# Batched trace of A·B: the uneven share of one load of B, 1,568 columns in five pieces instead of 800 in four

## The chip, the cores and the metric

The kernel runs on one core of one Trainium2 chip. The metric is the device time of the program in microseconds; the time before is 707.16 us, the median of three runs (707.16 to 707.89).

## The reference

For each of 8 pairs of 2176 x 2176 float32 matrices, the trace of the product is computed:

```python
B, N = 8, 2176
prod = np.matmul(a, b)                                    # a, b: [B, N, N] float32
traces = np.diagonal(prod, axis1=1, axis2=2).sum(axis=-1)
return traces.astype(np.float32)                          # [B]
```

The trace of A·B is the sum over all i, k of A[i, k] · B[k, i]. So no matrix product is needed: A is transposed, multiplied element by element with B, and summed.

## The kernel before

The rows of a matrix are cut into three groups: two of six rows a partition (6 x 128 rows each) and one of five (5 x 128). Partition p of a group holds r consecutive rows. Three large buffers in bfloat16 receive the loads: `a_six` (both groups of six of A), `b_six` (the same of B) and `five` (the group of five, of A and of B in turn). `at` holds A transposed, in the layout of B.

All large loads are issued from GpSimd's queue (POOL) by the helper `fetch` (line 179), and they cast float32 to bfloat16 on the way. For each batch `n` the order is: the five rows of A into `five`, the twelve rows of A into `a_six`, the five rows of B into `five`, the twelve rows of B into `b_six`. POOL waits before an issue until the buffer is free. `product` (line 188, 211) counts the products on VectorE that have been read out of `five` and `b_six`; `made` counts the tiles that TensorE has transposed.

TensorE transposes A in tiles into three PSUM slots (L253 and L256). ScalarE (L295) copies three of every four tiles into `at`, VectorE (L319) the fourth. VectorE then multiplies `at` with the five and with the six rows of B and sums along the free axis (L308), in place. The loop over `n` in which VectorE does this waits for `b6_full[n]`, the full count of the loads of `b_six` of that batch (line 329). The last batch is different: its B comes in ten pieces, part of which TensorE multiplies (L282) and sums on the diagonal.

Each load of 128 partitions is spread over the core's 16 DMA engines, and each engine counts 1 on the load's semaphore when its part is done.

The load of `b_six` in the fourth batch (`UNEVEN = 3`) differs from the others. `cut` is the place in each row block of 6 x 2176 = 13056 columns where the last `NARROW` columns begin. The load up to `cut` covers all 128 partitions; the last `NARROW` columns of both groups are loaded in pieces, one for each number in `COUNTS`, which is how many partitions it covers. The sum of `COUNTS` is 128, and all pieces together load the same bytes as the one load in the other batches:

```python
if n == UNEVEN:
    cut, p0 = SIX * N - NARROW, 0
    fetch(d_b6, dst[:, :, :cut], src[:, :, :cut])
    for count in COUNTS:
        p1 = p0 + count
        fetch(d_b6, dst[p0:p1, :, cut:], src[p0:p1, :, cut:])
        p0 = p1
else:
    fetch(d_b6, dst, src)
b6_full.append(d_b6.count)
```

Of the kernel before, what the change touches and what calls it, by code (L numbers as in the profile page):

```python
# [21 lines left out]
def kernel(  # L22
# [12 lines left out]
    TWICE = 2 * SIX  # L35
    assert TWICE + FIVE == NT
    LAST = BATCH - 1
    UNEVEN, NARROW, COUNTS = 3, 800, (13, 70, 9, 36)
    assert sum(COUNTS) == P and UNEVEN < LAST

    bf16 = mybir.dt.bfloat16
# [367 lines left out]
```

## Time and profile before

| | before |
|---|---|
| median of 3 runs | 707.16 us (707.16, 707.89, 707.16) |
| profiled execution | 707.1 us, span 705.3 us |
| HBM read | 303.04 MB, 430 GB/s over the span |
| VectorE busy | 385.8 us (55%) |
| ScalarE busy | 204.9 us (29%) |
| TensorE busy (matmul) | 198.9 us (28%) |
| GpSimd busy | 28.1 us (4%) |
| load of the twelve rows of B, uneven batch | 6128.0 KB and pieces of 40.6, 218.8, 28.1 and 112.5 KB |

The span runs from the first to the last instruction of the program; the profiled execution's time is 1.8 us longer. The DMA view counts the bytes as written, in bfloat16, which is half of the bytes read. Its "GB/s" row cuts the window that is asked for into 40 slices and gives for each the bytes of the packets that start in it, so in a short window a single packet of one DMA engine can be seen. Its packet line counts the packets below certain sizes; a packet of 4 bytes is the one with which an engine counts on a semaphore. Queue q0 carries the loads issued from POOL; q8 and q14 carry instructions.

### The profile page before, as it was taken

The page shows a single profiled execution, that of the slowest core. Times are in us where ns is not written, and L with a number is a line of the kernel's source. Part 1 is how long each engine was busy: PE and PEld are TensorE (multiplying, and loading weights), DVE is VectorE, ACT ScalarE, POOL GpSimd, SP SyncE. Part 2 cuts the span into 40 slices and gives each one's busy share as a digit, 9 for nine tenths or more (in the row PEclk, how much of TensorE's full clock was granted, in tenths as well). Part 3 has the DMA queues.
Part 4 walks back from the last instruction along what each step waited for, and adds up shares of the span by engine and source line. Part 5 has one row for each costly group of instructions (what it writes and reads, how often), then busy time and mean ns, then how long its engine had stood idle before and what let it go on. Part 6 is the DMA issues. An engine that isn't in the chain of part 4 may idle for free. (4 is left out here: it accounts for less than half of the span.)

```text
span 705.3 us, 3828 instructions
## 1 busy us (share of the span) xinstructions
PE 198.9 (28%) x1563; PEld 180.1 (26%) x1563; DVE 385.8 (55%) x98; ACT 204.9 (29%) x162; POOL 28.1 (4%) x51
## 2 busy tenths in 40 slices
PE   0335003450124501344013440134301253014604
PEld 0334002340123401244012430134301243014503
DVE  0105488154871549715396163961639616395497
ACT  1427002470024700346004450044500445005800
POOL 1000000000000000020000000000000000002000
PEclk9759555795556855568556785557855568556956
DMA  9999999999999999999999999999999999999998
GB/s 237 213 217 207 231 205 215 216 225 213 220 223 213 207 218 223 215 212 219 221 214 218 220 214 214 227 213 211 218 219 215 216 223 214 214 227 215 206 216 164
DMA packets 8231, 152.14 MB, mean 216 GB/s; under 512 B 930, under 2 KB 1314, under 8 KB 1698
## 3 DMA queue, kind: packets, MB, share of 16 engines
q0 software_dynamic: 8080, 150.97, 99.9%
q10 hardware_dynamic: 144, 1.11, 0.5%
q8 instruction: 2, 0.03, 0.0%
q14 instruction: 3, 0.02, 0.0%
q1 hardware_dynamic: 2, 0.00, 0.0%
HBM read 303.04 MB, written 0.00 MB: 430 GB/s over the span
## 5 line engine op out<-in xcount | busy, mean ns | idle before, releaser
L295 ACT COPY at<-aT 128x1536 bf16<-128x1536 bf16 (+3 forms) x160 | 202.5, 1357 | 459.2 <-DVE sums L308 356.6
L308 DVE CUSTOM_DVE_ANT_0 at<-at,b_six 128x26112 bf16<-128x26112 bf16 (+1 forms) x11 | 219.1, 19937 | 83.0 <-DMA b_six<-in_b_dram 83.0
L319 DVE COPY at<-aT 128x1536 bf16<-128x1536 bf16 (+1 forms) x48 | 80.1, 1669 | 209.8 <-PE aT L253 157.4
L253 PE MATMUL aT<-identity,five 128*128 128x128 f32 x240 | 54.3, 415 | 368.4 <-PEq L250 368.4
L253 PEld LDWEIGHTS aT<-identity,five 128*128 128x128 f32 x240 | 46.7, 220 | 374.3 <-issue 374.3
L253 PE MATMUL aT<-identity,a_six 128*128 128x128 f32 x576 | 89.2, 316 | 96.5 <-PEq L250 96.4
L253 PEld LDWEIGHTS aT<-identity,a_six 128*128 128x128 f32 x576 | 82.3, 205 | 102.8 <-issue 102.8
L308 DVE CUSTOM_DVE_ANT_0 at<-at,five 128x10880 bf16<-128x10880 bf16 (+3 forms) x10 | 84.9, 8493 | 15.9 <-ACT at L295 14.3
L256 PE MATMUL aT<-identity,a_six 128*128 128x128 bf16 x480 | 33.5, 219 | 10.9 <-PEq L250 10.7
L256 PEld LDWEIGHTS aT<-identity,a_six 128*128 128x128 bf16 x480 | 29.4, 118 | 14.8 <-issue 14.8
L180 POOL DMA_DIRECT2D five<-in_b_dram x13 | 7.2, 565 | 291.1 <-PE aT L256 291.1
L256 PE MATMUL aT<-identity,five 128*128 128x128 bf16 x200 | 17.2, 261 | 0.4 <-PEq L250 0.4
L256 PEld LDWEIGHTS aT<-identity,five 128*128 128x128 bf16 x200 | 16.9, 133 | 0.9 <-issue 0.6
L180 POOL DMA_DIRECT2D five<-in_a_dram x8 | 4.7, 584 | 291.5 <-DVE sums L308 290.7
L282 PE MATMUL trace_ps<-five,at 128*128 128x128 bf16 x55 | 5.3, 275 | 27.6 <-DMA five<-in_b_dram 27.6
L282 PEld LDWEIGHTS trace_ps<-five,at 128*128 128x128 bf16 x55 | 4.8, 127 | 28.5 <-issue 27.6
L180 POOL DMA_DIRECT2D b_six<-in_b_dram x15 | 9.5, 649 | 36.9 <-DVE sums L308 36.9
L180 POOL DMA_DIRECT2D a_six<-in_a_dram x9 | 6.1, 681 | 0.0
L157 DVE CAST five<-b_six 128x1088 bf16<-128x1088 f32 x1 | 0.7, 727 | 5.7 <-DMA b_six<-in_a_dram 5.7
L284 PE MATMUL aT<-at 128*128 128x512 bf16 x8 | 3.0, 521 | 0.0
L156 ACT CAST five<-b_six 128x1088 bf16<-128x1088 f32 x1 | 1.1, 1098 | 3.3 <-DMA b_six<-in_a_dram 3.3
L156 ACT ACT_TABLE_LOAD x1 | 1.3, 1283 | 1.1 <-PEq L393 1.1
(17 smaller groups left out, 5.2 us busy)
## 6 DMA issues: line engine op xcount, KB each, us to landing
a_six<-in_a_dram POOLq DMA_DIRECT2D x7, 6528.0 KB, 54.7
b_six<-in_b_dram POOLq DMA_DIRECT2D x6, 6528.0 KB, 52.3
five<-in_b_dram POOLq DMA_DIRECT2D x7, 2720.0 KB, 22.0
five<-in_a_dram POOLq DMA_DIRECT2D x7, 2720.0 KB, 24.4
a_six<-in_a_dram POOLq DMA_DIRECT2D x2, 3264.0 KB, 46.0
b_six<-in_b_dram POOLq DMA_DIRECT2D x4, 1632.0 KB, 34.5
b_six<-in_b_dram POOLq DMA_DIRECT2D x1, 6128.0 KB, 48.6
five<-in_a_dram POOLq DMA_DIRECT2D x1, 2176.0 KB, 14.7
```

Source lines behind the costliest of these rows:

```text
L156: nc.scalar.copy(out=five[:, 0, :middle], in_=words[:, :middle])
L157: nc.vector.tensor_copy(out=five[:, 0, middle:], in_=words[:, middle:])
L180: reached = count.by(gp.dma_start(out=dst, in_=src), 16)
L253: last = pe.transpose(ps[:, place, :], src, identity32)
L256: last = pe.transpose(ps16[:, place * P:(place + 1) * P], src, identity16)
L282: ins = pe.matmul(trace_ps, x, y, start=w is real[0], stop=w is real[-1])
L284: pe.matmul(slots[0][:, 0:4, :], x, y, start=True, stop=True)
L295: ins = act.copy(out=dst, in_=view(slots[t % SLOTS]))
L308: return dve.tensor_tensor_reduce(out=x if out is None else out, in0=x, in1=y, scale=1.0, scalar=0.0, op0=MUL, op1=ADD, accum_out=acc,)
L319: ins = dve.tensor_copy(out=dst, in_=view(slots[t % SLOTS]))
```

## The change

One line is changed. The part of the uneven load that goes in pieces is 1,568 columns wide instead of 800, and there are five pieces of 13, 39, 14, 42 and 20 partitions instead of four of 13, 70, 9 and 36. POOL issues one load more in this batch; the bytes loaded are the same, and the instructions of all other engines are the same.

```diff
-    UNEVEN, NARROW, COUNTS = 3, 800, (13, 70, 9, 36)
+    UNEVEN, NARROW, COUNTS = 3, 1568, (13, 39, 14, 42, 20)
```

## Prediction

> **What bounds the kernel now.** I read the page first, then the chain of waits, then the DMA view in windows of one to three microseconds.
>
> ```profile
> span 705.3 us, 3828 instructions
> DMA  9999999999999999999999999999999999999998
> DMA packets 8231, 152.14 MB, mean 216 GB/s; under 512 B 930, under 2 KB 1314, under 8 KB 1698
> HBM read 303.04 MB, written 0.00 MB: 430 GB/s over the span
> ```
>
> The 16 DMA engines are busy in every slice, and no compute engine is over 55% on the page. A load casts: the 152.14 MB counted are the bfloat16 bytes written, half of what is read. 216 / 16 = 13.5 GB/s is one DMA engine's pace in written bytes. All of `a` and `b` has to come through these engines, so the time can change only by what an engine is given, or by engines left idle.
>
> ```profile
> 649.66 44.74 DMA five<-in_b_dram
> ...
> 701.70 0.91 PE trace_ps L282 x13
> ...
> 702.64 0.29 DVE diagonal L308
> ...
> 703.23 0.15 DVE result L362
> ```
>
> The chain of waits ends with the last loads of `five`, the last 13 matmuls, and a short tail of fixed steps. A load has landed when its slowest engine has finished. So the end is set by the DMA engine that finishes last, not by the mean of the sixteen.
>
> The DMA view shows the engines' standing. In a window of 2.0 us its GB/s row has slices of 0.05 us. Where one load ends and the next begins, each engine's first packet of the next load shows as 522 (26,112 B in 50 ns; 1045 is two engines, 1567 three, 2089 four). The three windows start at 277.0, 363.9 and 451.2 us, always at the step from `five` to `a_six`, in the fourth, fifth and sixth batch.
>
> ```profile
> GB/s 0 522 522 0 522 522 0 2089 1045 1045 1045 522 0 0 0 0 0 0 0 0 0 0 0 0 0 0 0 0 0 0 0 0 522 0 0 0 0 0 0 0
> ```
> ```profile
> GB/s 0 0 0 0 522 0 0 0 522 0 0 522 0 0 522 0 0 1045 0 0 522 0 1045 522 1567 522 522 0 522 0 0 0 0 0 0 0 0 0 0 0
> ```
> ```profile
> GB/s 0 0 0 0 522 0 0 0 0 0 0 522 0 522 0 0 0 1045 0 1045 0 0 1045 1045 1045 522 522 0 522 0 0 0 0 0 0 0 0 0 0 0
> ```
>
> First row: fifteen engines pass in slices 1 to 11, one alone in slice 32. The mean of the sixteen is slice 8.6, that is 277.45 us; the laggard passes at 278.63, 1.17 us behind the mean. Second row, after the uneven loads: one engine early in slice 4 (364.13), four between 8 and 17, ten between 17 and 26, the last in 28 (365.33). The mean is 364.89, so the laggard is 0.43 behind it, and the next engine (slice 26) 0.10 ahead of the laggard. Third row: mean 452.22, last engine still in slice 28, 0.41 behind. The standing is kept.
>
> Where the laggard comes from is in the windows 66.9 to 67.9 and 698.3 to 699.4 us (first two lines, then the third):
>
> ```profile
> q0 software_dynamic: 4, 0.10, 49.8%
> q8 instruction: 1, 0.02, 5.8%
> ```
> ```profile
> q8 instruction: 1, 0.02, 5.5%
> ```
>
> A fetch of instructions rides on one DMA engine: 5.8% of 16 engines for 1.0 us is 0.93 us of one. It makes one engine late from 67 us on. A second one (5.5% of 1.1 us x 16, 0.97 us) comes just before the end. So before gives two engines less: the laggard, and the one that is early in the second row and gets its fetch at 698.
>
> **The change, part by part.** First, who gets what. In the fourth batch the last columns of `b_six` are loaded in pieces of rows; I call one row's share (two groups) a unit. Before, a unit is 2 x 800 x 2 B = 3,200 B written, at 13.5 GB/s 0.237 us of an engine; after, 2 x 1,568 x 2 B = 6,272 B, 0.465 us. An even spread is 8 units an engine. The window 349.6 to 352.8 us, and for comparison the one from 277.0:
>
> ```profile
> DMA packets 416, 0.76 MB, mean 237 GB/s; under 512 B 144, under 2 KB 400, under 8 KB 400
> ```
> ```profile
> DMA packets 32, 0.42 MB, mean 209 GB/s; under 512 B 16, under 2 KB 16, under 8 KB 16
> ```
>
> An ordinary load ends with 16 tiny packets, one an engine. Here there are 144 for five loads: 80 of that kind and 64 more. If 13, 70, 9 and 36 rows run on 13, 14, 9 and 12 engines (1, 5, 1 and 3 rows each), the idle engines are 3, 2, 7 and 4; one tiny packet for each packet they do not carry (two a row) makes 3x2 + 2x10 + 7x2 + 4x6 = 64. That fits exactly. The 256 left between 512 B and 2 KB are the pieces' 128 rows x 2.
>
> If each piece starts at the engine behind the last one's, numbered from the first piece's start, engines 0 to 3 get 7 units, 4 to 10 get 9, 11 and 12 get 5, and 13 to 15 get 9. So two engines move ahead by 3 units, four by 1, and ten fall back by 1. That is the second row: one early, four, ten, and the laggard, which came from 1.17 to 0.43 behind the mean, 0.74, against 3 x 0.237 = 0.71 computed. This is the reading I take.
>
> The same with 13, 39, 14, 42 and 20 rows: 13, 13, 14, 14 and 10 engines with 1, 3, 1, 3 and 2 rows each. Engines 0 to 5 get 8 units, 6 and 7 get 7, 8 and 9 get 9, 10 to 12 get 7, and 13 to 15 get 9. The turns add to 48 before and 64 after, both whole rounds of 16. The two engines with the fetches, 11 and 12, are relieved by one unit of 0.465 us instead of three of 0.237.
>
> So the laggard is later than before by 0.711 - 0.465 = 0.246 us. Is it still last? The ten get at most one unit more: 0.465 instead of 0.237, 0.228 later. Their last was 0.10 ahead of the laggard in the second row and stays 0.12 ahead. The early engine comes 0.246 later as well, and after its fetch stood at -0.77 + 0.97 = 0.20 behind the mean, below the laggard's 0.43. So the laggard ends last and carries all of its 0.246 us into the end.
>
> Second, one load more. From the first of the three rows to the second, the mean moves by 364.89 - 277.45 = 87.44 us; from the second to the third, with the same bytes and no pieces, by 87.33. The four pieces cost the mean engine 0.11 us together, 0.03 each. I take 0.03 for the fifth; its bounds are 0 and the 0.11 of all four. Packets per piece stay two a row.
>
> POOL issues one load more:
>
> ```profile
> L180 POOL DMA_DIRECT2D b_six<-in_b_dram x15 | 9.5, 649 | 36.9 <-DVE sums L308 36.9
> ```
> ```profile
> 301.83 3.12 POOL L180 DMA_DIRECT2D b_six<-in_b_dram  x5
> 341.79 0.59 POOL L180 DMA_DIRECT2D five<-in_a_dram  x1 [36.84 <-DVE sums L308]
> 342.37 0.73 POOL L180 DMA_DIRECT2D a_six<-in_a_dram  x1
> 387.42 0.58 POOL L180 DMA_DIRECT2D five<-in_b_dram  x1 [44.32 <-PE aT L256]
> ```
>
> That is 0.65 us on POOL, which then waits 36.84 us for a product; the pieces are issued by 305 and run at about 350. Nothing. Without that wait it would cost 0.65 us of POOL, and still no DMA time while loads are queued.
>
> Third, the product of `b_six` waits for the last piece, 0.27 us later:
>
> ```profile
> 352.98 27.36 DVE L308 CUSTOM_DVE_ANT_0 at<-at,b_six 128x26112 bf16<-128x26112 bf16 x1 [11.48 <-DMA b_six<-in_b_dram]
> ```
>
> It releases the copies out of PSUM and so, over PE, the issue at 387.42. What is queued then is the load of `a_six` issued at 342.37, which begins at the step in the second row (364.89) and is 128 x 26,112 elements x 2 B = 6.68 MB, at 216 GB/s 30.9 us: to 395.8. The issue has 8 us in hand, so 0.27 us hide in it.
>
> Sum: 0.246 + 0.03 = 0.27 us. Before's profiled execution took 707.1 us (span 705.3); after's would take 707.4. Against the median of the runs shown, 707.16, that is 707.43. **Forecast 707.4 us**, 0.04% more. A measurement of this kernel can tell about 0.2% from no change, 1.4 us, so this counts as no change.
>
> **The rivals.**
>
> *A, the pieces start elsewhere.* If the first piece begins at another engine than in before's profile, the laggard can fall among those with 9 units: from 0.711 relieved to 0.465 loaded, 1.18 us, with 0.03 for the fifth piece 708.4. For it: one of before's three runs took 707.89, 0.73 more than the others, about the 0.71 that a laggard without relief would cost. Against it: whole rounds in both. [...] Chance 0.08, of which 0.02 beyond 0.2%.
>
> *B, the pattern suits the fetches better.* If the engine that ends last is one of 6, 7 or 10, it goes from one unit too many to one too few, 0.70 us earlier. What can be won is bounded: the laggard is 0.43 behind the mean, and the two fetches still to come move the mean by 0.97 / 16 = 0.06 and by less; with all sixteen level at the end 0.3 to 0.4 us are won. That is 706.8 to 706.9. Against it: the 1.17 of the first row came down by 0.74, so the laggard is one of the two relieved engines. Chance 0.07.
>
> *C, slower: a small load costs its own latency.* If an engine could not go on to the next piece until the last was confirmed, each piece would show its round trip. The only bare one in the trace is the result's:
>
> ```profile
> 703.41 0.32 SPq L367 DMA_DIRECT2D out_dram<-result  x1
> ```
>
> The span ends at 705.3, so it takes at most 1.9 us. Once more is 707.16 + 0.27 + 1.9 = 709.3, slower by 0.3%. It decides if the queue drains between pieces. Against it: four pieces cost 0.11 us together. [...] Chance 0.04.
>
> *D, the change does not do what it says.* If 39 rows ran on 3 engines with 13 rows each (39 is 3 x 13), these would have 13 + (128 - 39) / 16 = 18.6 units, 10.6 above 8, 4.9 us: 712.1. Against it: the 64 tiny packets, which fit only the widest split. Chance 0.03.
>
> **How the numbers follow.** The forecast has 0.76, A 0.08, B 0.07, C 0.04, D 0.03; 0.02 are left for a gain that no row shows. C, D and A's 0.02 are slower by over 0.2%: 0.09. Faster 0.02, the same 0.89. The range runs from B's 706.9 to 708.3, short of A: it takes in the bounds of the fifth load and a run like 707.89. C, D, A and the unseen gain, 0.17, lie outside.
>
> **What would show it.** In after's profile the window of the pieces has 96 + 64 = 160 tiny packets (3x2 + 3x6 + 2x2 + 2x6 + 6x4 = 64 again). The row at the step near 364 us has its last engine about 0.68 us behind the mean (0.43 + 0.25) instead of 0.43, and the early one about 0.5 ahead instead of 0.77. The mean moves by 87.47 us from the step near 277. I am wrong if the last engine is not later at that step, if it is by over 1 us (A), if the mean shifts by over 0.5 us (C), or if the fetch windows show their packets at other times.

## The result, and the profile after

After takes 708.97 us, the median of 16 runs (708.30 to 709.37); before, with 16 runs now, 707.92 us (707.03 to 708.15). The ratio is 1.0016 with an interval of 1.0009 to 1.0023, so the change costs about 1.1 us. The forecast was 707.4 us, in a range up to 708.3. Before's runs fall on two values, near 707.1 and near 708.0, so the 707.16 us from which the forecast started, the median of three runs, was its lower value. Both profiled executions lie at the lower end of their kernel's runs, 707.1 for before and 708.3 for after, 1.2 us apart; what after's other runs, most of them near 709, lose beyond that no trace shows.

The page of after:

```profile
span 706.5 us, 3828 instructions
DMA  9999999999999999999999999999999999999998
DMA packets 8247, 152.14 MB, mean 215 GB/s; under 512 B 946, under 2 KB 1074, under 8 KB 1714
HBM read 303.04 MB, written 0.00 MB: 429 GB/s over the span
```

The same bytes, and 946 small packets instead of 930: 16 more, as many as end one load in the window from 277.0 us. The window from 347.8 to 353.5 us, which holds the end of the uneven load and all five pieces, has 160 of them: 96 end six loads, and 64 are left for the pieces' idle engines, as computed. The DMA row is as full as before; the same bytes just took longer (215 GB/s against 216).

The standing of the engines, at the same two steps as before (windows from 277.0 and from 364.7 us, 0.05 us a slice; 522 is one engine's first packet of the next load, the 435 belongs to the load that ends):

```profile
GB/s 0 0 0 522 1045 522 522 1045 1045 522 522 522 522 0 522 522 0 0 0 0 0 0 0 0 0 0 0 0 0 0 522 0 0 0 0 0 0 0 0 0
```
```profile
GB/s 0 0 0 0 435 522 0 0 522 522 0 0 0 522 522 0 522 0 522 522 0 0 0 0 522 0 522 0 522 522 1045 522 0 0 0 0 0 522 0 0
```

The mean engine passes at 277.50 and at 365.78, 88.28 us apart. Before needed 87.44 with pieces and 87.33 without. So after's pieces cost the mean engine 0.95 us, where 0.14 was forecast (0.94 by the exact starts of the packets, which the table below uses). The last engine is 1.02 us behind the mean at the first step and 0.80 at the second, where 0.68 was forecast. Compared with before at the second step, by the exact starts, the mean is 0.89 us later and the last engine 0.33 further behind it, 1.22 together: that is the 1.2 us between the profiled executions.

Where the 0.9 us lies can be seen in the packets of the pieces. Two windows of after, 349.0 to 349.8 and 350.3 to 351.3 us, in which only packets of pieces (3,136 B) and tiny ones start:

```profile
DMA packets 61, 0.16 MB, mean 200 GB/s; under 512 B 10, under 2 KB 10, under 8 KB 61
## 3 DMA queue, kind: packets, MB, share of 16 engines
q0 software_dynamic: 61, 0.16, 103.8%
```
```profile
DMA packets 86, 0.19 MB, mean 188 GB/s; under 512 B 26, under 2 KB 26, under 8 KB 86
## 3 DMA queue, kind: packets, MB, share of 16 engines
q0 software_dynamic: 86, 0.19, 121.5%
```

In the first, 51 packets of pieces took 103.8% x 16 x 0.8 us = 13.3 us with the tiny ones at some 0.02 us each, so about 0.26 us a packet. In the second, 60 packets and 26 tiny ones took 19.4 us, 0.315 us for each packet of a piece. Over all 256 packets of the pieces the trace has 252 ns at the least and 538 ns at the most, and what exceeds 252 ns adds up to 0.66 us for the mean engine. Before's 256 packets of 1,600 B all took 139 or 140 ns. Packets of the next load that run beside the last pieces are slow too: 15 of 21,760 B exceed the usual 1.62 us, by up to 0.79, and add 0.32 us for the mean engine. The two together, 0.98 us with overlaps not taken off, cover the 0.84 by which after's pieces cost more than before's (0.94 less 0.10).

The product on VectorE that waits for the last piece starts at 354.76 us instead of 352.98, 1.8 us later and not 0.27, but the cover held:

```profile
354.76 27.36 DVE L308 CUSTOM_DVE_ANT_0 at<-at,b_six 128x26112 bf16<-128x26112 bf16 x1 [13.18 <-DMA b_six<-in_b_dram]
```
```profile
301.88 3.60 POOL L180 DMA_DIRECT2D b_six<-in_b_dram  x6
...
390.06 0.56 POOL L180 DMA_DIRECT2D five<-in_b_dram  x1 [46.90 <-PE aT L256]
```

The issue behind it comes at 390.06 instead of 387.42, with the load of `a_six` queued until about 396.7, which is the mean engine's 365.78 and the 30.9 us that the prediction computed for this load.

### The profile page after: what moved, and what is told of

It is laid out like the page before. It is cut to its first block, busy times and chain, and to the rows that moved or that the text cites. A ratio compares the mean times of both kernels' runs of the same rounds, so it can differ in the third digit from the quotient of the medians.

```text
span 706.5 us, 3828 instructions
## 1 busy us (share of the span) xinstructions
PE 199.1 (28%) x1562; PEld 180.4 (26%) x1563; DVE 385.8 (55%) x98; ACT 205.0 (29%) x162; POOL 28.4 (4%) x52
```

## The experiments

Theory P, formed after the result: engines that write to crowded neighbouring rows of SBUF at the same time hold each other up, which the rows of the pieces of 39, 42 and 20 bring about. Rivals: W, pieces that are 1,568 columns wide are slow by themselves; H, the rows read from HBM make them slow; and the count of loads (rival C of the prediction). "Lost to the pieces" below is the mean engine's time from the step near 277 to the one near 364 us, less 87.33; "last" is the distance of the last engine from the mean at the second step. Both are from the first packets of the load of `a_six` at these steps in the trace, to 0.01 us.

| kernel | profiled, us | median, us | longest piece packet, ns | lost to the pieces, us | last, us |
|---|---|---|---|---|---|
| before | 707.1 | 707.92 | 140 (1,600 B) | 0.10 | 0.46 |
| after | 708.3 | 708.97 | 538 (3,136 B) | 0.94 | 0.79 |
| 1,568 columns, old counts | 707.23 | 707.36 | 253 (3,136 B) | 0.09 | 0.52 |
| 800 columns, new counts | 707.77 | 707.74 | 140 (1,600 B) | 0.12 | 1.01 |
| after, other rows | 707.78 | 707.93 | 562 | 0.56 | 0.60 |
| no pieces | 707.61 | 707.61 | none | -0.04 | 1.10 |
| other rows, written side only | 707.81 | 708.02 | 498 | 0.54 | 0.66 |
| other rows, read side only | 707.99 | 708.95 | 445 | 0.60 | 0.71 |
| writes spread over SBUF | 707.33 | 707.51 | 253 | 0.12 | 0.63 |
| before, tiny plain loads | 707.23 | 707.20 | 140 | 0.15 | 0.46 |
| after, rows spread, right data | 707.46 | 708.12 | 253 | 0.14 | 0.73 |
| before, turned by four | 708.36 | 708.07 | 140 | 0.14 | 1.21 |
| after again | 708.01 | one run | 464 | 0.71 | 0.74 |
| before, turned by eight | 707.98 | 708.07 | 140 | 0.16 | 0.87 |

The two right columns carry over to the end: their sum, less before's 0.10 and 0.46, gives the profiled difference from before's 707.1 us to within 0.15 us, in all kernels but those turned by four and by eight, which come last in this section.

**The width alone.**

```diff
-    UNEVEN, NARROW, COUNTS = 3, 1568, (13, 39, 14, 42, 20)
+    UNEVEN, NARROW, COUNTS = 3, 1568, (13, 70, 9, 36)
```

> 1,568 columns, but in before's four pieces of 13, 70, 9 and 36 rows: the width alone. Theory P (engines that write into crowded neighbouring rows of SBUF block each other, which the 39, 42 and 20 rows bring): the packets of the pieces stay near 252 ns, the mean engine loses at most 0.2 us to the pieces, the last engine is one with 9 units, about 0.6 us behind the mean; about 0.2 us over before. Theory W (pieces of 6,272 B read are slow by themselves, whatever their rows): slow packets stay, the mean loses about 0.8 us as in after, 0.9 to 1.2 us over before.

No slow packet: 253 ns at most, 0.09 us lost, 707.23. One engine is 1.60 us ahead of the mean at the second step, about what three units of 0.465 us less make. The runs are a ratio of 0.9996 to before (0.9987 to 1.0005). W falls: packets as wide as after's run at full pace with before's rows. Neighbouring rows alone are not enough for slow packets either, since the piece of 36 rows, three to an engine if before's 64 tiny packets are read as in the prediction, has them too.

**The counts alone.**

```diff
-    UNEVEN, NARROW, COUNTS = 3, 1568, (13, 39, 14, 42, 20)
+    UNEVEN, NARROW, COUNTS = 3, 800, (13, 39, 14, 42, 20)
```

> 800 columns in after's five pieces of 13, 39, 14, 42 and 20 rows: the counts alone. Theory P: the same crowding with packets half as long, so slow packets among the 256 and 0.1 to 0.4 us lost by the mean; the laggard is relieved by one unit of 0.237 us only and stands 0.9 us behind the mean: 0.6 to 0.9 us over before. Theory W: no slow packet, the mean loses 0.14 us, and only the laggard's 0.47 us counts: 0.5 us over before.

No slow packet here either, against P, which expected some; 0.12 us lost by the same five loads in the same rows. So the slow packets need both the new rows and the longer packets, and the number of loads costs nothing like 0.8 us. The laggard is as forecast for one unit of 0.237 us: from 1.25 behind the mean at the first step to 1.01. That laggard, and not slow packets, makes most of the 0.67 us over before.

**Other rows for the same pieces**, then the written and the read side alone (the last two put the data into the wrong rows).

```diff
-                        p1 = p0 + count
-                        fetch(d_b6, dst[p0:p1, :, cut:], src[p0:p1, :, cut:])
-                        p0 = p1
+    # rows 81, 0, 94, 39, 108 for the pieces of 13, 39, 14, 42, 20: d0 and s0, d0 alone, s0 alone
+                        fetch(d_b6, dst[d0:d0 + count, :, cut:], src[s0:s0 + count, :, cut:])
```

> After's widths, counts and order of pieces, so the same engines get the same units, but the pieces cover other rows: 13 at 81, 39 at 0, 14 at 94, 42 at 39, 20 at 108, so that the 42 rows lie in the middle and no two of them are 32 apart in one half of the partitions. Theory P: the fourth piece is no longer slow, the mean loses less than 0.4 us instead of 0.8; 0.3 to 0.7 us over before. Theory W: as after, 1.0 to 1.2 us over before.

> As the run with the other rows, but only where the pieces are written changes (SBUF rows 81, 0, 94, 39, 108 for the pieces of 13, 39, 14, 42, 20); they read after's rows of HBM. The data then stand in the wrong rows. Theory P (crowding among the engines that write to SBUF): the slow packets and the mean's loss are those of that run, 0.6 us, 707.8 in the profiled execution. Theory H (the rows read from HBM make the packets slow): as after, 0.98 us lost by the mean and 708.3.

> The other half: the pieces are written to after's rows of SBUF (0, 13, 52, 66, 108) and read the rows 81, 0, 94, 39, 108 of HBM, so the data stand in the wrong rows. Theory P: as after, 0.98 us lost by the mean, 708.3 in the profiled execution. Theory H: 0.6 us lost and 707.8.

The rows matter: 0.56 us lost instead of 0.94, and a median of 707.93. That is more than P's 0.4, and slow packets remain (562 ns at the most; in order of start the first is the 153rd of the 256, so from the piece of 42 rows on). In the profiled executions the two halves hardly differ (0.54 and 0.60). Over the runs they do: with the written side moved the median is 708.02, beside 707.93 for both; with the read side moved it is 708.95, beside after's 708.97. That speaks for the written side. A single profile did not decide it: after again lost 0.71 us where its first profile lost 0.94, so of the 0.38 between 0.94 and 0.56 up to 0.23 can be a difference between executions.

> After once more, for a second profile: how much the slow packets vary from execution to execution. Theory P: again packets of over 400 ns in the last pieces, the mean loses 0.6 to 1.0 us to the pieces, and the profiled execution takes 707.9 to 708.4.

**The writes spread out.** Each piece reads after's rows, but four of them write every third row of SBUF; the piece of 13 goes to a tile of its own.

```diff
+                    to = (
+                        scratch, dst[1:118:3, :, cut:], dst[62:104:3, :, cut:],
+                        dst[0:126:3, :, cut:], dst[2:62:3, :, cut:],
+                    )
```

> After's pieces read after's rows of HBM, but four of them are written to every third row of SBUF (39 to rows 1, 4, ... 115; 14 to 62, 65, ... 101; 42 to 0, 3, ... 123; 20 to 2, 5, ... 59) and the one of 13 rows to a tile of its own, so that neighbouring engines no longer write neighbouring rows. The data then stand in the wrong rows. Theory P: no or few packets over 270 ns, the mean loses at most 0.3 us to the pieces, the last engine is about 0.7 us behind the mean, and the profiled execution takes 707.3 to 707.6. Theory H: 96 or so slow packets, 0.98 us lost and 708.3.

This decides between the two sides. Nothing is changed on the read side, and no packet takes over 253 ns; 0.12 us are lost, and the profiled execution takes 707.33 (10 runs, median 707.51). It shows that the rows written matter; how the engines meet there it does not show. Then with the right data, each piece every third row on both sides:

```diff
+                    for some in (
+                        slice(117, 127, 3), slice(103, 128, 3), slice(0, 115, 3),
+                        slice(61, 101, 3), slice(2, 126, 3), slice(1, 59, 3),
+                    ):
+                        fetch(d_b6, dst[some, :, cut:], src[some, :, cut:])
```

> After with the right data: each piece is every third row of both HBM and SBUF (117 to 126, 103 to 127, 0 to 114, 61 to 100, 2 to 125, 1 to 58), the piece of 13 rows as two of 4 and 9, so that each engine gets the same units as in after. Theory P: no packet of the pieces over 270 ns, 0.2 us lost by the mean, the last engine 0.6 to 0.7 us behind the mean, 707.3 to 707.5 in the profiled execution, 1 us less than after. If reading rows that are three apart costs something, slow packets come back and it is over 707.8.

The profiled execution takes 707.46, in the range expected; its steps (windows from 277.1 and 364.2) and its packets from 350.3 to 351.3 us, to be held against after's:

```profile
GB/s 0 0 0 1045 2089 2089 0 1045 522 522 0 0 522 0 0 0 0 0 0 0 0 0 0 0 0 0 0 0 0 0 0 522 0 0 0 0 0 0 0 0
```
```profile
GB/s 0 1045 0 522 0 0 0 522 0 0 0 522 1045 522 0 522 0 0 0 0 1045 0 1045 522 522 0 0 0 0 522 0 0 0 0 0 0 0 0 0 0
```
```profile
DMA packets 94, 0.21 MB, mean 213 GB/s; under 512 B 26, under 2 KB 26, under 8 KB 94
## 3 DMA queue, kind: packets, MB, share of 16 engines
q0 software_dynamic: 94, 0.21, 110.0%
```

The mean moves from 277.49 to 364.96, 87.47 us, the very figure forecast for after, and the last engine is 0.72 behind it. In the window 68 packets of pieces, not 60, took 17.6 us with 26 tiny ones: 0.25 us each. Its median of 708.12 is 0.85 us under after's, but no better than before's: ratio 1.0007 (0.9998 to 1.0016). Nor is it under the 707.93 of the run with other rows, whose profile has slow packets. So the spread removes the slow packets in the profiled execution; over the runs, all that is seen is that the medians with after's written rows lie near 709.0 and those with the same pieces in other rows between 707.5 and 708.1. The kernel has six loads instead of four, so rival C's price for a load is excluded once more.

**What the pieces are worth, and where they start.**

```diff
-    UNEVEN, NARROW, COUNTS = 3, 1568, (13, 39, 14, 42, 20)
+    UNEVEN, NARROW, COUNTS = -1, 1568, (13, 39, 14, 42, 20)
```

> No uneven load at all: the fourth batch's rows of B come in one load like the others. What the relief is worth in before: the laggard keeps its 1.15 us behind the mean to the end instead of 0.43, less 0.11 us that four pieces cost the mean: 0.6 us over before under every theory. If it is far less, it is not the laggard that sets the end.

707.61, 0.5 us over before's profiled 707.1: near what was expected. The laggard stays 1.10 us behind the mean. The runs lie between 707.47 and 707.76, and before's two values were not seen without the pieces. Over the runs the relief is worth nothing that can be told: most of before's runs lie near 708.0, and the ratio is 0.9996 (0.9987 to 1.0005). Two tiny loads that should turn the pieces' start:

```diff
+                    fetch(turn, scratch[0:4, :], b[0][0:4, 0:64])
                     for count in COUNTS:
...
+                    fetch(turn, scratch[4:16, :], b[0][4:16, 0:64])
```

> Before, with a tiny load of 4 rows (128 B each) ahead of its pieces and one of 12 rows behind them: if each load starts at the engine behind the last one's, the pieces start four engines further on and the laggard falls among those with 9 units instead of 5. Then it stands 1.17 + 0.24 = 1.4 us behind the mean after the pieces, and the profiled execution takes 0.95 us more than before's 707.1, 708.0 or 708.1 with the two tiny loads, as do most of before's own unprofiled runs. If the loads always start at the same engine, nothing moves and it is 707.2.

That missed: 0.46 us behind and 707.23, so in this execution a load of this form did not turn the start. Yet nine of ten runs lie at 707.1 to 707.3, where before has 2 of 31 beside it; why is open. With tiny loads of the pieces' own form, `scratch[0:4], src[0:4, :, 0:64]` and 4 to 16, and then 8 and 8 rows:

> Before, turned by a tiny load of the pieces' own form (4 rows, two groups of 64 columns) ahead of them and one of 12 rows behind them. In the run with plain tiny loads the laggard stayed among the engines with 5 units. If loads of this form share one place from which the next starts, the laggard now gets 9 units and stands 1.4 us behind the mean after the pieces: 708.0 to 708.1 in the profiled execution. If the place does not move, 707.2 to 707.3.

> Before, turned by eight engines: a tiny load of the pieces' form of 8 rows ahead of them and one of 8 rows behind. Theory S (the pieces start at one of two places eight engines apart, from execution to execution, and the second puts the laggard among those with 9 units, which is why before takes 707.1 or 708.0): in the profiled execution, if it starts where before's did, the laggard gets 9 units and stands 1.4 us behind the mean after the pieces, 708.0 to 708.2; if it starts at the other place, the turn undoes it, 0.45 us and 707.2. Over the runs the two values change places or mix. If the time of 708.0 has another cause, the profiled execution gives some third value, such as 707.6 with a laggard at 0.9.

Both take the laggard out of the group with 5 units, and cost 1.3 and 0.9 us in the profiled execution. But the laggard's place is not the one that was expected: turned by four, the last engine goes from 1.36 to 1.21 us behind the mean, where one unit more would make 1.6. The step near 364 us after the turn by eight (window from 363.9):

```profile
GB/s 0 0 522 435 0 0 435 0 0 0 522 0 0 522 1045 0 0 0 0 0 522 522 522 1045 522 522 0 522 522 0 0 0 0 0 0 522 0 0 0 522
```

The last engine is 0.89 us behind the mean, not 1.4: 1.10 at the first step, by the exact starts, less some 0.2, one unit relieved and not one added. The prediction's own count has this: turned by eight, engine 11 gets engine 3's 7 units (and 12 gets 9), so the expectation miscounted if the laggard is 11. The time is 707.98 all the same, before's second value. At that step the last engine is only 0.5 us later than before's, of the 0.9. The rest must fall behind it, and the trace bears out that the fetch near 699 us no longer lands on an engine that is early. In this trace, as in before's and after's, an engine's next packet mostly starts 18 or 19 ns before its last one ends, or 1 ns before where that was a tiny one. Followed back so, with one candidate at every step, the engine of the fetch at 698.74 us passed the step near 626 us 0.08 us behind the mean, where the last engine was 0.83 behind. With the fetch's 0.97 us it stands about 1.0 behind. In the kernel turned by four the same tracing finds it 0.07 ahead, so about 0.9 behind after the fetch; there the last engine stood 1.21 behind at the step near 364 us, and some 0.4 of the 1.3 us stays without a cause.

## Why the prediction was wrong

**What bounds the kernel** held: busy DMA engines, and the last of them sets the end. In after its passing at the second step is 1.22 us later than before's, and the profiled execution 1.2 us longer.

**Who gets what** held where it could be checked without slow packets: the 64 tiny packets, and the laggard's relief by one unit (1.25 to 1.01 at 800 columns, computed 0.237; 1.18 to 0.73 at 1,568 with spread rows, computed 0.465). In after itself it did not show: the last engine came from 1.04 to 0.79 behind the mean, 0.25 instead of 0.465. That it ended only 0.12 from the forecast 0.68 is partly luck, as after's laggard stood less far behind at the first step (1.04, before 1.15). Slow packets that do not hit all engines alike would explain the difference; no run shows it engine by engine.

**The step that failed** is "Second, one load more ... I take 0.03 for the fifth; its bounds are 0 and the 0.11 of all four". I took the cost of the pieces for a cost of each load and carried it over, and let each packet run at 13.5 GB/s because before's packets do. The term measured 0.95 us for all pieces, where 0.14 was forecast, and what it consists of is slow packets, which the sum did not have. The bounds were too narrow, because the nearest row, before's pieces, had packets half as long; at that length even the new rows show nothing (800 columns, new counts: 140 ns).

**The base** was off as well. The forecast of 707.43 added 0.27 us to 707.16, but before's median over 16 runs is 707.92. Of the 1.54 us by which after's 708.97 exceeds the forecast, 0.76 come from there and 0.78 from the change, which costs 1.05 us in the medians and not 0.27. Either alone would have stayed in the range (708.19 and 708.21).

**The rivals.** C named the sign that came, a mean that shifts by over 0.5 us, but not the cause: five loads of 800 columns and six spread loads of 1,568 lose 0.12 and 0.14 us, and the packets themselves are long. None of the rivals had the rows that are written in it. The runs show that these matter: spread, the pieces have no packet over 253 ns. Why they matter, no run shows. A distance of 32 rows, which the run with other rows kept out of its piece of 42, was not shown to be the cause: packets of 562 ns remained, and before's 70 rows (13 to 82), which hold such pairs, ran 1,568 columns at 253 ns.

**A** was right that before has a second value 0.9 us higher, and the two turned kernels come to it (median 708.07). The mechanism priced there, the laggard with 9 units, did not show in their profiles; in the kernel turned by eight it was the later fetch that found no early engine. What before itself does in its slower runs no trace shows. **B** and **D** did not occur.

**The hidden steps.** POOL's issue and the later product cost nothing, though the product came 1.8 us later and not 0.27.

## What to carry to other kernels

When a load is cut into pieces of few rows, look not only at how many bytes each DMA engine gets but at which rows are written: interleaved rows (every third) took 1,568 columns at no more than 253 ns a packet where much the same pieces in neighbouring rows lost 0.6 to 0.8 us more (0.71 and 0.94, against 0.14). Pieces of 13, 70, 9 and 36 neighbouring rows lost no more than 0.09, so the profile has to tell which counts do. A price taken from short packets did not hold for long ones here (0.12 us lost at 800 columns, 0.94 at 1,568 in the same rows): look at the durations of the packets in the size that will run. Take the base, too, from enough runs to see whether they fall on one value or two. And where sixteen engines run side by side, the GB/s row of a window of 2 us at the step from one load to the next shows each one's standing, which is what a difference of 0.1% was made of here.

## What was not expected of the hardware

Packets of 3,136 B into neighbouring rows took up to 538 ns instead of 252, while packets of 1,600 B into the same rows took 140 ns at the most, and packets of 3,136 B into the rows of 13, 70, 9 and 36 took 253. Which rows make the packets slow was not separated. With pieces the time depends on the execution: before's runs lie near 707.1 or near 708.0, the kernel without pieces at 707.47 to 707.76 alone, and before with two tiny plain loads at 707.07 to 707.30 in nine of ten runs (707.20 in the median, ratio to before 0.9991, 0.9981 to 1.0000). Whether the pieces start at other engines from one execution to the next, and what sets it, is open.
